# Zero matmuls, a scheduler that follows TensorE's clock, and a new order of the early work in a hybrid encoder block

## The chip, the cores and the metric

The kernel runs on one core of a Trainium2 chip. The metric is the device time of one execution in microseconds (us). Each program is run several times and the median is given. TensorE (PE) does the matrix products, VectorE (DVE), ScalarE (ACT) and GpSimd (POOL) the elementwise work, and SyncE (SP) issues most transfers. The clock of PE that the chip grants has two levels here, 1.2 and 2.4 GHz; the profile gives it as a share, 0.50 or 1.00.

## What is computed

One layer of a streaming encoder on 1024 tokens of width 1024, in float32. The reference, cut to what matters:

```python
def block(x, mem, ...):
    h = rms_norm(x, g_mix)
    cq, ckv, krope, gate, u = split(h @ w_in)          # 256, 128, 32, 512, 512 columns
    q = rms_norm(cq, g_cq) @ w_uq                      # 8 heads, 64 + 32 rotary
    k, v = split(rms_norm(ckv, g_ckv) @ w_ukv)         # 8 heads, 64 each
    a = block_causal_attention(rope(qk_norm(q)), rope(qk_norm(k, krope)), v)
    r = rg_lru(u, conv_w, ...) * gelu(gate)            # conv, gates, linear scan in time
    x = x + concat(rms_norm(a), rms_norm(r)) @ w_out
    x = x + mem_cross_attention(rms_norm(x), rms_norm(mem), ...)
    return x + hier_moe(rms_norm(x), ...)              # 32 experts, 2 of 8 in the best group
```

The recurrent part, which the text comes back to, is `a = exp(-8 r softplus(-lam))`, `b = sqrt(1 - a*a) * (i * xc)` and the scan `h[t] = a[t] h[t-1] + b[t]`, with `r` and `i` sigmoids of two small block-diagonal products of `xc`.

## The kernel before, in words

A float32 product is made of three matmuls on values split into a high and a low part (`mm3`): names that end in `h` and `l` are such parts, and ACT makes the high part while DVE makes the low one (`evac_split`). The tokens are cut in eight tiles `t` of 128; attention takes them in four pairs `pr`. The stages are:

- the in-projection: `zb` gives `z` (the latents q and kv and the rotary key) for every tile, `pr` the eight column blocks of the recurrent part (`rnn_x`, `rnn_u`);
- `prep(t)`: `pcT` transposes a tile of `z`, `pk`, `pq` and `pv` are the up-projections, then the norm of q and k in `qs` and `kn`, the rotation of `qs` by the tables `tab`, and `pqT`, eight transposes each of `kn` and of `qs`, which give `kTh`, `kTl`, `qTh` and `qTl`;
- `step(s)`: one step of attention over a head of a pair. `at_max` forms scores `pS` and their row maxima `nm` on DVE; `at_row` transposes the maxima (`pnm`), which ACT writes to `nT` and a DMA puts into a row of `qT`; `at_exp` forms scores in the transposed form, `pST`, which ACT turns into `PT`; `at_pv` gives `po`, which DVE divides into `oa`; `at_out` norms a finished pair and transposes it (`poT`);
- `rnn_gates_end(c)`: the gate products `pg` of column block `c`, and behind them a chain over ACT and DVE (`ra`, `ri`, `tl`, `sq`), the scan, `gt` and the sum of squares; `rnn_ss` takes the sum of squares over the tokens by matmuls with ones (`pss`);
- the out-projection, cross-attention to the memory, the routing, and the experts, whose weights are loaded, split and multiplied.

The order of all that is not the order of the code. `body` runs the functions above once and records every operation in `Prog.ops`, with its engine, an assumed duration and what it depends on. The sequence of the recording is `PLAN`, a string of short names: `w` is `mla_w` (loads and splits of `w_uq` and `w_ukv`), `x`, `u` and `g` with a number are `rnn_x`, `rnn_u` and the gates of a column block, `z` is `mla_z`, `p` is `prep`, `s` is `step`, `q` is `rnn_ss`, `k` `mem_k`, `r` `rnn_out`, `o` `outproj_w`, `t` the out-projection of a token tile, `T` and `R` are `x1_T` and `x1_r`, the transposes and the row sums of the result, and `v` is `mem_v`. Then `Prog.order` makes a list schedule: it lets a clock run, and whenever an engine is free it takes the recorded operation with the lowest number that is ready and may start (`can`). An operation may not start when the tiles it opens do not fit: there are 49 large slots, 24 small ones, and 8 banks of PSUM (`CAPS`). `LAT` holds the assumed hand-over times between engines. What comes out is the instruction order of each engine, and the hardware then waits for the true dependences. The table `ON` says for which tiles an elementwise operation of `prep` is on DVE; the others are on POOL.

All instructions are issued by one helper (L156 before, L160 after the change), so the rows are told apart by the tiles they write and read.

Of the kernel before, what the change touches and what calls it, by code (L numbers as in the profile page):

```python
# [9 lines left out]
F32 = mybir.dt.float32  # L10
F32R = mybir.dt.float32r
BF = mybir.dt.bfloat16
# [6 lines left out]
P = 128  # L19
# [11 lines left out]
    LAT[_e, "SP"] = LAT["SP", _e] = 0.2  # L31


AHEAD, AHEAD_SPLIT, AHEAD_LOAD, AHEAD_MOE, THR = 30.0, 24.0, 30.0, 4.0, 3.0


# [74 lines left out]


class _Op:
    __slots__ = ("eng", "cost", "emit", "deps", "succ", "tiles", "i", "ahead", "wait", "dma", "keep", "t0", "thr", "port")


class Prog:
    def __init__(self, tc, pools):
        self.tc, self.pools, self.ops, self.direct = tc, pools, [], False
        self.ahead = AHEAD  # L120
        self.n = 0
        self.after = None
        self.hold = None
        self.fast = False

    def tile(self, kind, shape, dt, name):
        t = _Tile(kind, list(shape), dt, name)
# [15 lines left out]
    def op(self, eng, cost, fn, args, kw, outs, ins, dma=0.0):  # L143
        def emit():
            for v in outs + ins:
                if v.t.real is None:
                    self.alloc(v.t)
            a = [x.real() if isinstance(x, _View) else x for x in args]
            k = {}
            for n, x in kw.items():  # L150
                if isinstance(x, _View):
                    x = x.real()
                elif isinstance(x, tuple) and x and x[0] == "ix":
                    x = bass.IndirectOffsetOnAxis(ap=x[1].real(), axis=0)
                k[n] = x
            return fn(*a, **k)  # L156
        if self.direct:
            return emit()
        o = _Op()
        o.eng, o.cost, o.emit, o.dma, o.i = eng, cost, emit, dma, len(self.ops)  # L160
        o.ahead, o.deps, o.succ, o.tiles, o.keep, o.thr = self.ahead, {}, [], [], 0, 1e9


        src = [v for v in ins if v.t.kind not in ("p", "d") and _free(v) > 1]
        o.port = not dma and (eng == "POOL" or eng == "DVE" and (len(src) > 1 or self.fast))
        for w, vs in ((False, ins), (True, outs)):
            for v in vs:
                t = v.t
                if t.kind == "p":
                    box = (0, P, 0, 1 << 30)  # L170
                else:
                    box = (v.p0, v.p1, int(v.idx.min()), int(v.idx.max()) + 1)
                for (j, wj, bx) in t.acc:
                    if (w or wj) and j != o.i and box[0] < bx[1] and bx[0] < box[1] and box[2] < bx[3] and bx[2] < box[3]:
                        o.deps[j] = True
                if w:
# [12 lines left out]
        return o  # L189


    def order(self):
# [63 lines left out]
            return True  # L256

        held = []
        while len(result) < n:
            held.clear()  # L260
            progress = True
            while progress:
# [4 lines left out]
                for e in engs:  # L267
                    if free[e] > now + 1e-9 or not (ready[e] or e == "SP" and loads):
                        continue
                    tried, pick = [], None  # L270
                    while pick is None and ready[e] and len(tried) < 40:
                        i = heapq.heappop(ready[e])
                        if can(ops[i]):
                            pick = i
                            break
                        tried.append(i)
                    for i in tried:
                        heapq.heappush(ready[e], i)
                    if pick is None and e == "SP" and loads and can(ops[loads[0]]):
                        pick = heapq.heappop(loads)  # L280
                    if pick is None:
                        continue
                    o = ops[pick]
                    for t in o.tiles:
                        if t.kind in CAPS and id(t) not in have:
                            have.add(id(t))
                            live[t.kind] += 1
                            N[t.kind][f:t.first] += 1
                    started[pick] = True
                    o.t0 = now  # L290
                    result.append(o)
                    while f < n and started[f]:
                        f += 1
                    end = now + o.cost
                    if o.port:
# [13 lines left out]
            while fin and fin[0][0] <= now + 1e-9:  # L309
# [8 lines left out]
                for s in o.succ:  # L318
# [6 lines left out]
        self.makespan = now  # L325
        return result

    def flush(self):
# [28 lines left out]
class _PE(_Engine):  # L357
    def matmul(self, o, lhsT, rhs, start, stop, **kw):
        n = _free(o)
        dt = rhs.dt  # L360
        c = max(0.109, n / 2246.0 + 0.004) if dt == F32R else (2 * max(0.109, n / 1123.0) if dt == F32 else max(0.027, n / 2246.0))
        return self._do("matmul", (o, lhsT, rhs), dict(start=start, stop=stop, **kw), c)

    def transpose(self, o, i, ident):
        return self._do("transpose", (o, i, ident), {}, 0.109)


# [49 lines left out]
for _name, _w in [("g_mix", 8), ("conv_w", 16), ("conv_b", 4), ("b_rg", 4), ("b_ig", 4), ("lam", 4),  # L417
# [3 lines left out]
    _n += _w  # L421
NPAR = _n

ON = {"qr": 4, "kr": 4, "ke": 0, "tm": 0, "qc": 8}

PLAN = """w x0 x1 x2 u0 g0 u1 g1 u2 z g2 p0 x3 p1 u3 s0 p2 s1 s2 s3 p3 s4 s5 s6 p4 s7 s8 s9 p5 s10 s11 s12 g3 s13 s14 s15
    q s16 s17 s18 s19 s20 s21 p6 p7 s22 s23 s24 s25 s26 s27 s28 s29 s30 s31 s32 k s33 s34 s35 s36 o s37 r t3 t0 t2  # L430
    s38 t7 t1 R0 T0 T1 t5 T2 T3 t4 t6 v R1"""
NROW = 224 * P
FAR = 8192

# [1 line left out]
def body(tc, A, out_ap):  # L436
# [243 lines left out]
    for t in range(NT):  # L680
# [2 lines left out]
        z.append(z_t[:, t % 2, :])  # L683
        SC.activation(z[t], acc[t], AF.Copy, scale=rx[:, t:t + 1])
    row_bcast(Rb, rx)


    ord_ = prog.tile("d", [4 * P, SEQ], F32, "ord")
# [706 lines left out]
    for t in range(NT):  # L1395
# [3 lines left out]
        for k in range(KC):  # L1399
            PE.matmul(pX[k // 4][:, k % 4 * P:k % 4 * P + P], XN[t][:, k * P:(k + 1) * P], sel0[0][:, t, :],  # L1400
                      start=t == 0 and k % 4 == 0, stop=t == NT - 1 and k % 4 == 3, skip_group_check=True)


    idx = Cn([P, 32], I32, name="idx")
    gts = Cn([P, 64], F32, name="gts")
# [240 lines left out]
```

## Time and profile before

| | us |
|---|---|
| median of 3 runs | 1132.08 (1131.44 to 1136.94) |
| the profiled execution | 1131.79 |
| its span | 1129.8 |
| mean granted clock of PE | 0.980 |

The profile comes from one execution, in which the time from the first to the last instruction, the span, is 1129.8 us. A row of a timeline is: start in us from the span's start, duration, engine, line, operation, output and inputs by their names, shapes, and the number of instructions of that kind in a row; in brackets the idle time of the engine just before, and what ended it. Durations of PE's matmuls overlap, since they are pipelined: what a matmul costs is the distance to the next one's start. In the 40 slices of the page each digit is the busy share of 28.2 us in tenths.

### The profile page before, as it was taken

What the parts mean: (1) busy time and instruction counts of PE and PEld (TensorE: products, weight loads), DVE (VectorE), ACT (ScalarE), POOL (GpSimd) and SP (SyncE); (2) the same over time, 40 slices, a digit from 0 to 9 for tenths busy, and PEclk for the clock granted to TensorE, in tenths of its full rate; (3) what the DMA queues carried; (4) which work ended last, traced back from release to release, by engine and by line L of the source; (5) the groups of instructions that cost most, each with busy time, mean ns of one, the idle gap of its engine ahead of it and who ended that gap; (6) DMA issues with size and microseconds to landing.
All of it is one profiled execution on the core that took longest, in us unless ns stands there. A gap on an engine that the chain in (4) does not pass through costs nothing. (4 is left out here: it accounts for less than half of the span.)

```text
span 1129.8 us, 16959 instructions
## 1 busy us (share of the span) xinstructions
PE 1084.4 (96%) x6013; PEld 926.3 (82%) x6014; DVE 787.6 (70%) x1692; ACT 685.3 (61%) x1163; POOL 181.8 (16%) x231
## 2 busy tenths in 40 slices
PE   7999999899999999999999999999999999998993
PEld 7988778899998988898888889889888777775762
DVE  5567899858763713454764356676999999997982
ACT  6837866636554612433492334443888888987982
POOL 1100023203000000000000121024333223233111
PEclk9999999779999999999999998999999999999997
DMA  9401100000443120352235627448899999989991
GB/s 345 186 19 38 57 1 1 19 2 2 169 161 138 34 98 20 128 190 75 75 150 186 211 75 243 149 150 288 296 330 333 332 322 315 320 305 305 327 307 32
DMA packets 61220, 190.18 MB, mean 168 GB/s; under 512 B 11121, under 2 KB 11906, under 8 KB 61131
## 3 DMA queue, kind: packets, MB, share of 16 engines
q1 hardware_dynamic: 52058, 172.48, 42.6%
q0 software_dynamic: 9072, 16.58, 6.0%
q8 instruction: 48, 0.79, 0.3%
q14 instruction: 42, 0.34, 0.1%
HBM read 174.00 MB, written 31.46 MB: 182 GB/s over the span
## 5 line engine op out<-in xcount | busy, mean ns | idle before, releaser
L156 DVE TENSOR_TENSOR wel<-wer,weh 128x1024 fp32r<-128x1024 f32 x192 | 228.0, 1222 | 21.1 <-ACT weh L156 17.7
L156 ACT ACTIVATE weh<-wer 128x1024 fp32r<-128x1024 f32 x192 | 196.1, 1063 | 14.4 <-DMA wer<-in_w_dn 7.9
L156 PE MATMUL pgu<-wel,xgTh 128*128 128x512 f32 x256 | 107.1, 418 | 7.2 <-DVE wel L156 7.1
L156 PE MATMUL pgu<-weh,xgTh 128*128 128x512 f32 x256 | 103.2, 403 | 0.7 <-ACT weh L156 0.6
L156 PE MATMUL pgu<-weh,xgTl 128*128 128x512 f32 x256 | 101.5, 396 | 0.0
L156 POOL DMA_INDIRECT out<-y,idx x32 | 55.0, 1718 | 221.8 <-DMA out<-y,idx 67.4
L156 PE MATMUL py<-weh,heT 128*128 128x512 f32 x256 | 85.7, 395 | 1.3 <-ACT heT L156 1.1
L156 PE MATMUL po<-V,PT 128*128 128x65 f32 x576 | 73.4, 280 | 0.4 <-DVE qTl L156 0.4
L156 PEld LDWEIGHTS po<-V,PT 128*128 128x128 f32 x576 | 70.7, 199 | 0.7 <-DVE qTl L156 0.6
L156 PEld LDWEIGHTS pgu<-wel,xgTh 128*128 128x128 f32 x256 | 48.2, 188 | 25.5 <-DVE wel L156 16.8
L156 ACT ACTIVATE PT<-pST 128x512 f32<-128x512 f32 (+1 forms) x80 | 42.2, 558 | 38.0 <-PE pST L156 37.0
L156 ACT ACTIVATE junk<-x 128x512 f32<-128x512 f32 x32 | 20.2, 632 | 72.7 <-DVE x L156 44.5
L156 ACT ACTIVATE y<-py,gts 128x512 f32<-128x512 f32 x64 | 43.8, 687 | 29.0 <-PE py L156 26.5
L156 PEld LDWEIGHTS py<-weh,heT 128*128 128x128 f32 x256 | 48.0, 188 | 13.0 <-ACT heT L156 1.3
L156 PEld LDWEIGHTS pgu<-weh,xgTh 128*128 128x128 f32 x256 | 48.1, 188 | 11.3 <-ACT weh L156 1.5
L156 PEld LDWEIGHTS pgu<-weh,xgTl 128*128 128x128 f32 x256 | 48.3, 189 | 7.9 <-DVE xgTl L156 0.4
L156 PE MATMUL py<-wel,heT 128*128 128x512 f32 x128 | 50.7, 396 | 1.7 <-DVE wel L156 1.7
L156 DVE TENSOR_REDUCE nm<-pS 128x1 f32<-128x512 f32 (+3 forms) x96 | 50.4, 550 | 1.7 <-PE pS L156 1.7
L156 PE MATMUL px<-VWh,PXh 128*128 128x512 f32 x128 | 51.1, 399 | 0.0
L156 PE MATMUL px<-VWh,PXl 128*128 128x512 f32 x128 | 51.1, 399 | 0.0
L156 PE MATMUL pqx<-x1Tl,wqh 128*128 128x512 f32 x128 | 50.8, 397 | 0.0
L156 PE MATMUL pqx<-x1Th,wqh 128*128 128x512 f32 x128 | 50.7, 396 | 0.0
(369 smaller groups left out, 2972.4 us busy)
## 6 DMA issues: line engine op xcount, KB each, us to landing
wer<-in_w_gu SPq DMA_DIRECT2D x128, 512.0 KB
wer<-in_w_dn SPq DMA_DIRECT2D x64, 512.0 KB
wqr<-in_w_mq SPq DMA_DIRECT2D x16, 512.0 KB
xt<-in_x SPq DMA_DIRECT2D x8, 512.0 KB
wrr<-in_w_rnn SPq DMA_DIRECT2D x8, 512.0 KB
wkr<-in_w_mk SPq DMA_DIRECT2D x8, 512.0 KB
wor<-in_w_out SPq DMA_DIRECT2D x8, 512.0 KB
x<-in_x SPq DMA_DIRECT2D x8, 512.0 KB
```

The lines of the kernel that those rows point to most:

```text
L156: return fn(*a, **k)
```

## The change

Four things change. A tile of zeros (`fil`, 128 x 128 bf16) and a PSUM tile `pfil` are made, and one matmul of them stands behind the z stage, one at the end of the routing; between the two the planner may repeat the first where PE has found nothing that may start. The planner counts the columns that PE works on (`cols`, four times for float32) in stretches of its own clock; it doubles PE's assumed durations in a stretch that follows one with few of them. `ON["kr"]`, the product of `kn` by its norm, goes from 4 to 6, so it is on DVE for tiles 4 and 5 too. And `PLAN` has another order: `x2` ahead of `w`, `z` ahead of `g1`, `t5` ahead of `t2`, `T0` ahead of `R0`. The core of the diff:

```diff
-        while len(result) < n:
+        win, act, half, slow = 0, {}, False, 0
+        recent = []
+        done = 0
+        while done < n:
...
+                    if e == "PE":
+                        while (win + 1) * WINDOW <= now:
+                            half = act.get(win, 0.0) < LOW * WINDOW
+                            win += 1
+                            slow += half
                     if pick is None:
+                        if e == "PE" and self.fill and started[self.fill[0].i] and not started[self.fill[1]]:
...
+                            if sum(x[1] for x in recent) < KEEP * WINDOW:
+                                d = self.fill[0]
+                                result.append(d)
...
                         continue
...
                     end = now + o.cost
+                    if e == "PE":
+                        end += o.cost * half
...
-ON = {"qr": 4, "kr": 4, "ke": 0, "tm": 0, "qc": 8}
-PLAN = """w x0 x1 x2 u0 g0 u1 g1 u2 z g2 p0 x3 p1 u3 s0 p2 s1 s2 s3 p3 s4 s5 s6 p4 s7 s8 s9 p5 s10 s11 s12 g3 s13 s14 s15
+ON = {"qr": 4, "kr": 6, "ke": 0, "tm": 0, "qc": 8}
+PLAN = """x2 w x0 x1 u0 g0 u1 z g1 u2 g2 p0 x3 p1 u3 s0 p2 s1 s2 s3 p3 s4 s5 s6 p4 s7 s8 s9 p5 s10 s11 s12 g3 s13 s14 s15
...
-    s38 t7 t1 R0 T0 T1 t5 T2 T3 t4 t6 v R1"""
+    t2 s38 t7 t1 T0 R0 T1 T2 T3 t4 t6 v R1"""
...
+    fil = Cn([P, P], BF, name="fil")
+    V.memset(fil, 0.0)
+    pfil = prog.tile("p", [P, 512], F32, "pfil")
+    PE.matmul(pfil[:, :P], fil, fil, start=True, stop=True)
+    d = prog.ops[-1]
+    prog.fill = [d, 0]
...
+    prog.fill[1] = len(prog.ops)
+    PE.matmul(pfil[:, :P], fil, fil, start=True, stop=True)
```

What the change makes of the order of the instructions, at the places that the prediction speaks of (an instruction, its output and inputs with the numbers of the buffers, and the size of the output):

On PE, in the early attention, at the transposes of tile 1 (`kn_1216` and `qs_1244` before, `kn_1220` and `qs_1248` now). Before:

```order
L156 MATMUL pqT_1446<-C_69,kn_1216 99x128 x4
L156 MATMUL pqT_1452<-C_69,kn_1216 99x128 x4
L156 MATMUL pq_1410<-wuql_456,cT_1383 128x384
L156 MATMUL pq_1410<-wuqh_444,cT_1383 128x384
L156 MATMUL pq_1420<-wuqh_434,cT_1383 128x384
...
L156 MATMUL pv_1435<-wukvh_460,cT_1383 128x512
L156 MATMUL pk_1475<-wukvh_460,cT_1399 128x512
L156 MATMUL pk_1475<-wukvl_472,cT_1399 128x512
L156 MATMUL pqT_1480<-C_69,qs_1244 99x128 x4
L156 MATMUL pqT_1486<-C_69,qs_1244 99x128 x4
```

With the change, from the second zero matmul on:

```order
L160 LDWEIGHTS fil_80
L160 MATMUL pfil_554<-fil_80 128x128
L160 MATMUL pS_256_1386<-kTh_1341,qTh_1368 128x128
...
L160 MATMUL pqT_1448<-C_69,kn_1220 99x128 x4
L160 MATMUL pqT_1458<-C_69,kn_1220 99x128 x4
L160 MATMUL pq_1415<-wuqh_435,cT_1388 128x384
L160 MATMUL pq_1415<-wuqh_443,cT_1388 128x384
L160 MATMUL pq_1415<-wuql_456,cT_1388 128x384
L160 MATMUL pqT_1472<-C_69,qs_1248 99x128 x4
L160 MATMUL pqT_1479<-C_69,qs_1248 99x128 x4
L160 MATMUL pq_1415<-wuqh_443,cT_1388 128x384
```

Of the up-projections between the two groups of transposes all but three now come behind the second.

On PE behind the gate products of the last column block (`pg`). `kn_1653` and `qs_1878` before are `kn_1788` and `qs_1885` now. Before:

```order
L156 MATMUL pS_433_2078<-kTh_1345,qTh_1724 128x256
L156 MATMUL pS_433_2078<-kTh_1670,qTh_1724 128x256
L156 MATMUL pST_2083<-qTh_1716,kTh_1337 128x256
...
L156 MATMUL pqT_2133<-C_69,kn_1653 99x128 x4
L156 MATMUL pqT_2138<-C_69,kn_1653 99x128 x4
L156 MATMUL pS_446_2144<-kTh_1345,qTh_1724 128x256
...
L156 MATMUL pqT_2206<-C_69,qs_1878 99x128 x4
L156 MATMUL pqT_2212<-C_69,qs_1878 99x128 x4
L156 MATMUL pnm_2218<-C_69,nm_2029 4x128
```

With the change:

```order
L160 MATMUL pS_438_2095<-kTh_1349,qTh_1735 128x256
L160 MATMUL pS_438_2095<-kTh_1687,qTh_1735 128x256
L160 MATMUL pqT_2104<-C_69,kn_1788 99x128 x4
L160 MATMUL pqT_2112<-C_69,kn_1788 99x128 x4
L160 MATMUL pqT_2123<-C_69,qs_1885 99x128 x4
L160 MATMUL pqT_2129<-C_69,qs_1885 99x128 x4
L160 MATMUL pST_2138<-qTh_1721,kTh_1341 128x256
...
L160 MATMUL pST_2173<-qTh_1721,kTl_1698 128x128
L160 MATMUL pnm_2186<-C_69,nm_1863 4x128
L160 MATMUL pST_2189<-qTh_1721,kTh_1341 128x256
```

Both groups of transposes now stand ahead of the 24 `pST`, and the first `pnm` behind them; a second `pnm` (from `nm_2038`) follows nine `pST` later.

On DVE in the same place, with the change (`ri` by `tl` and the operation that writes `sq_2098`, the scan, are the last of the gate chain):

```order
L160 TENSOR_TENSOR qs_1885<-qs_1885 128x8x32
L160 TENSOR_TENSOR kTl_1964<-pqT_2112,kTh_1946 99x4x128
L160 TENSOR_TENSOR ri_2073<-ri_2073,tl_2051 128x1024
...
L160 SCALAR_TENSOR_TENSOR sq_2098<-ra_2025,ri_2073 128x1024
L160 SCALAR_TENSOR_TENSOR qTl_1994<-pqT_2123,colq_76,qTh_1975 99x4x128
...
L160 TENSOR_TENSOR gt_1427<-sq_2098,gt_1427 128x1024
...
L160 TENSOR_REDUCE nm_1863<-pS_437_2091 128x1
L160 TENSOR_TENSOR sq_922<-sq_922,sq_2098 128x1024
...
L160 TENSOR_REDUCE nm_2038<-pS_438_2095 128x1
```

The maxima `nm` from which the two `pnm` are made stand behind the scan, the two `qTl` and `gt`; before, the first of the pair (`nm_2029`) stood ahead of the scan.

## Rows read from the trace of the kernel before

**Rows 1.** The page: PE's total, and busy tenths and granted clock in slices.

```profile
PE 1084.4 (96%) x6013; PEld 926.3 (82%) x6014; DVE 787.6 (70%) x1692; ACT 685.3 (61%) x1163; POOL 181.8 (16%) x231
...
PE   7999999899999999999999999999999999998993
...
PEclk9999999779999999999999998999999999999997
```

**Rows 2.** Stretches: length, busy us (instructions) by engine, PE's granted clock, DMA share, GB/s.

```profile
150.00:180.00 30.00, 26.80 (x175) 23.40 (x174) 29.32 (x77) 24.37 (x42) 7.91 (x23) 1.00 0.00 1
205.80:213.40 7.60, 6.17 (x55) 6.01 (x53) 5.85 (x11) 7.36 (x11) 1.52 (x7) 1.00 0.00 0
213.40:237.40 24.00, 22.79 (x104) 21.99 (x105) 15.02 (x43) 8.11 (x19) 2.04 (x7) 0.50 0.06 23
```

**Rows 3.** Timeline of PE, 212 to 243 us.

```profile
213.46 0.58 PE L156 MATMUL pST<-qTh,kTh 97*128 97x256 f32 x1 [1.49 <-ACT PT L156]
...
215.55 2.03 PE L156 MATMUL pqT<-C,qs 128*99 128x128 f32 x8 [0.44 <-POOL qs L156]
...
224.80 3.41 PE L156 MATMUL pss<-ones,sq 128*128 128x1 f32 x16
...
228.43 0.41 PE L156 MATMUL pST<-qTh,kTh 97*128 97x256 f32 x1
...
230.88 3.19 PE L156 MATMUL po<-V,PT 128*128 128x65 f32 x14
...
236.86 0.41 PE L156 MATMUL pST<-qTh,kTh 97*128 97x256 f32 x1
...
238.44 1.72 PE L156 MATMUL po<-V,PT 128*128 128x65 f32 x14
...
240.76 0.28 PE L156 MATMUL pST<-qTh,kTh 97*128 97x256 f32 x1
...
242.11 0.61 PE L156 MATMUL po<-V,PT 128*128 128x65 f32 x4
```

**Rows 4.** Timeline of PE, 159 to 164 us.

```profile
159.90 0.50 PE L156 MATMUL pk<-wukvh,cT 128*128 128x512 f32 x1 [2.51 <-DVE cT L156]
...
160.58 1.03 PE L156 MATMUL pqT<-C,kn 128*99 128x128 f32 x8
...
163.44 1.04 PE L156 MATMUL pqT<-C,qs 128*99 128x128 f32 x8
```

**Rows 5.** Timeline of POOL, near 163 us.

```profile
162.91 0.21 POOL L156 COPY qs<-mrow 128x24 f32<-128x24 f32 x1 [2.27 <-DVE qs L156]
```

**Rows 6.** Timeline of DVE, one row near 183 us, then 206 to 220 us.

```profile
182.79 0.69 DVE L156 TENSOR_TENSOR kn<-kn,rqk 128x512 f32<-128x512 f32 x1
...
206.64 1.30 DVE L156 SCALAR_TENSOR_TENSOR tl<-sq,tl 128x1024 f32<-128x1024 f32 x1 [1.06 <-ACT sq L156]
...
208.07 0.68 DVE L156 TENSOR_REDUCE nm<-pS 128x1 f32<-128x512 f32 x1
...
209.28 0.42 DVE L156 TENSOR_TENSOR qs<-qs,tab 128x256 f32<-128x256 f32 x1
...
211.53 1.23 DVE L156 TENSOR_TENSOR ri<-ri,tl 128x1024 f32<-128x1024 f32 x1 [0.90 <-ACT tl L156]
...
213.21 2.28 DVE L156 TENSOR_TENSOR_SCAN sq<-ra,ri 128x1024 f32<-128x1024 f32 x1
217.48 1.60 DVE L156 SCALAR_TENSOR_TENSOR qTl<-pqT,colq,qTh 99x512 fp32r<-99x512 f32 x2 [2.00 <-ACT qTh L156]
219.00 1.22 DVE L156 TENSOR_TENSOR gt<-sq,gt 128x1024 f32<-128x1024 f32 x1
```

**Rows 7.** Timeline of ACT, 205 to 210 us.

```profile
205.08 0.59 ACT L156 ACTIVATE PT<-pST 128x512 f32<-128x512 f32 x1
205.56 1.06 ACT L156 ACTIVATE sq<-ra 128x1024 f32<-128x1024 f32 x1
...
209.15 1.28 ACT L156 ACT_TABLE_LOAD   x1
```

More of the change, by code (lines that the diff above doesn't have):

```diff
@@ L31 @@
     LAT[_e, "SP"] = LAT["SP", _e] = 0.2
+WINDOW, LOW, KEEP = 3.413, 0.34, 0.5
 AHEAD, AHEAD_SPLIT, AHEAD_LOAD, AHEAD_MOE, THR = 30.0, 24.0, 30.0, 4.0, 3.0
@@ L113 @@
 class _Op:
-    __slots__ = ("eng", "cost", "emit", "deps", "succ", "tiles", "i", "ahead", "wait", "dma", "keep", "t0", "thr", "port")
+    __slots__ = ("eng", "cost", "emit", "deps", "succ", "tiles", "i", "ahead", "wait", "dma", "keep", "t0", "thr", "port", "cols")
 class Prog:
@@ L124, in __init__ @@
         self.fast = False
+        self.cols = 0
+        self.fill = None
     def tile(self, kind, shape, dt, name):
@@ L161, in op @@
         o.ahead, o.deps, o.succ, o.tiles, o.keep, o.thr = self.ahead, {}, [], [], 0, 1e9
+        o.cols = self.cols if eng == "PE" else 0
         src = [v for v in ins if v.t.kind not in ("p", "d") and _free(v) > 1]
@@ L280, in order @@
                         pick = heapq.heappop(loads)
-                    if pick is None:
+                    if e == "PE":
[3 more added lines that the diff above has]
+                            slow += half
+                    if pick is None:
+                        if e == "PE" and self.fill and started[self.fill[0].i] and not started[self.fill[1]]:
+                            while recent and recent[0][0] < now - WINDOW:
+                                recent.pop(0)
+                            if sum(x[1] for x in recent) < KEEP * WINDOW:
+                                d = self.fill[0]
+                                result.append(d)
+                                c = d.cost * (2 if half else 1)
+                                free[e] = now + c
+                                recent.append((now, d.cols / 2400.0))
+                                act[win] = act.get(win, 0.0) + d.cols / 2400.0
+                                progress = True
                         continue
@@ L291, in order @@
                     result.append(o)
+                    done += 1
                     while f < n and started[f]:
@@ L294, in order @@
                     end = now + o.cost
+                    if e == "PE":
+                        end += o.cost * half
+                        recent.append((now, o.cols / 2400.0))
+                        act[win] = act.get(win, 0.0) + o.cols / 2400.0
                     if o.port:
@@ L324, in order @@
                         heapq.heappush(soon, (rt[s], s))
-        self.makespan = now
+        self.makespan, self.slow = now, slow
         return result
@@ L361, in matmul @@
         c = max(0.109, n / 2246.0 + 0.004) if dt == F32R else (2 * max(0.109, n / 1123.0) if dt == F32 else max(0.027, n / 2246.0))
+        self.prog.cols = n * (4 if dt == F32 else 1)
         return self._do("matmul", (o, lhsT, rhs), dict(start=start, stop=stop, **kw), c)
     def transpose(self, o, i, ident):
+        self.prog.cols = _free(o)
         return self._do("transpose", (o, i, ident), {}, 0.109)
@@ L422 @@
 NPAR = _n
-ON = {"qr": 4, "kr": 4, "ke": 0, "tm": 0, "qc": 8}
-PLAN = """w x0 x1 x2 u0 g0 u1 g1 u2 z g2 p0 x3 p1 u3 s0 p2 s1 s2 s3 p3 s4 s5 s6 p4 s7 s8 s9 p5 s10 s11 s12 g3 s13 s14 s15
-    q s16 s17 s18 s19 s20 s21 p6 p7 s22 s23 s24 s25 s26 s27 s28 s29 s30 s31 s32 k s33 s34 s35 s36 o s37 r t3 t0 t2
-    s38 t7 t1 R0 T0 T1 t5 T2 T3 t4 t6 v R1"""
+ON = {"qr": 4, "kr": 6, "ke": 0, "tm": 0, "qc": 8}
+PLAN = """x2 w x0 x1 u0 g0 u1 z g1 u2 g2 p0 x3 p1 u3 s0 p2 s1 s2 s3 p3 s4 s5 s6 p4 s7 s8 s9 p5 s10 s11 s12 g3 s13 s14 s15
+    q s16 s17 s18 s19 s20 s21 p6 p7 s22 s23 s24 s25 s26 s27 s28 s29 s30 s31 s32 k s33 s34 s35 s36 o s37 r t3 t0 t5
+    t2 s38 t7 t1 T0 R0 T1 T2 T3 t4 t6 v R1"""
 NROW = 224 * P
```

## The prediction

> **What bounds the kernel now.** I read the page's engine list first, then its slices, then the stretches where a slice shows less than a full TensorE, and there the order of waits engine by engine. PE is busy 1084.4 of 1129.8 us, and in its slices almost every digit is a 9 [rows 1]: it is the bound nearly everywhere, so a change can win only where PE idles or where its clock is low. The PEclk digits show one place: the 7s near 212 to 240 us. The table of stretches takes it apart [rows 2]: from 213.4 to 237.4 the granted clock is 0.50 (the lower level, 1.2 GHz) with PE busy 22.79 of 24.00 us. At the upper level (2.4 GHz) the same matmuls would take half, 11.4 us; that is the largest thing an order of the early work could win here, 1.0% of the span. The 7.6 us ahead of the fall had PE busy 6.17 us only, and the last wait before it is 1.49 us for ACT's PT [rows 2, 3]. The clock came back at 237.4, half a microsecond into a pST group, behind po, poT and pS matmuls without a gap [rows 3].
>
> The page's second loss is in 150 to 180 us, where PE is busy 26.80 of 30 and DVE 29.32: DVE is the bound there [rows 2]. All times below are in the clock of the profiled execution of before, which took 1131.79 us, 0.3 us under the median of the runs shown. The point up to which I compare is the pST at 236.86 [rows 3]; the order on PE behind it is the same for a long way. About 0.5%, 5.7 us, is what a measurement of this kernel can tell from no change: "same" is 1126.4 to 1137.7.
>
> **Zero matmuls.** The planner may repeat the first one when PE has work that may not start, but the order of the built program holds only the two written by hand. The first stands at about 46 us, behind the z stage; the one that ends the filling is ready at once and goes out the first time PE has nothing else, at about 154 us. None stands in a later wait. So the change does not do what its words say: it does not fill PE's idle time, and what remains of it is the order. A 128-column bf16 matmul is not in the trace. From above: eight 128-column transposes last 1.03 us together [rows 4], 0.13 each, two make 0.26. From below it is nothing, where PE waits anyway; no gain, since neither stands near the waits ahead of the fall. I take 0.2, the upper end, for these two places have PE busy. The one PSUM bank of eight that the two hold between them costs nothing I can place: PE is at 9 in every slice from the second to the seventh [rows 1].
>
> **Start and later moves.** One load of the recurrent weights goes one place ahead on SP's queue, and their splits on ACT go ahead of two evacuations of z. The in-projection matmuls fill slices two to five completely [rows 1], so this costs nothing; without that cover it would show as idle time in those slices. The out-projection of token tile 5 and the transposes of x1 behind it move as a block in a stretch where PE is full and at full clock [rows 1]: nothing.
>
> **Stage 155 to 199 us.** The kn products of tiles 4 and 5 move from POOL to DVE, 0.69 us each [rows 6], so DVE, full here, has 1.4 us more to do. And PE reaches the transposes of qs of tile 1 earlier. In before it does the eight of kn at 160.58, then some ten up-projection matmuls, and the eight of qs at 163.44 [rows 4], just when POOL's copy into qs has ended (162.91 + 0.21) [rows 5]. In the new order only three pq matmuls stand between the two. They take some 0.6 us, so PE arrives at 162.0 and waits to 163.4: +1.4. The matmuls that covered this come later, where they cover nothing that was not covered. From below it is nothing, if a later DVE wait was longer by as much and shrinks; from above 3, that wait and DVE's two products one behind the other (1.4 + 1.4 = 2.8). I take +1.4.
>
> **Stage of the gates, 199 to 237 us.** Here the order moves most. In before 24 pST stand ahead of the transposes of the next tile's kn, and 12 more and two po groups ahead of those of qs, which run at 215.55 after 0.44 us of wait [rows 3]. In the new order the transposes of kn and qs stand directly behind the gate matmuls and three pS groups, with the 24 pST behind them. PE gets through kn at about 205.6. But qs is not ready: its chain goes over ACT and DVE. ACT's sq ends at 206.6 in before; one PT of about 0.5 us ahead of it goes [rows 7], so 206.1. Then DVE, word for word in the new order: tl to 207.3, nm to 207.9, qs by tab to 208.3, one kTl (like the kn product, about 0.6) to 208.9, the add on qs to 209.3 [rows 6]; POOL's copy 0.2 [rows 5] and hand-overs: 209.6. **PE idles 4.0 us there**, more than twice the 1.49 us behind which the clock fell in before. So I expect it to fall earlier.
>
> From 209.6 the eight transposes (2.03 at the low clock) and the 24 pST in front of pnm (12 took 228.43 to 230.88, 2.45) are done by 216.5 [rows 3]. That costs nothing by itself, since DVE's chain to pnm is longer: kTl to 210.0, ri by tl 1.2 (its tl comes from ACT behind a table load of 1.28, in time [rows 7]), nm 0.6, the scan 2.2 to 214.2, qTl twice 1.6, gt 1.2 to 217.0, and two nm with small ones 1.5: 218.5 [rows 6]. The first pnm waits for it; the second stands behind one more 1.2 us sum and an nm, and comes at **220.6** (in before the pair of pnm was spread over 217 to 223).
>
> What PE still has from there to the common point, priced at the low clock: three pST 0.6, seven po 3.0 (the row of 14 halves, 230.88), then everything that before does from 224.80 to 236.86 (pss, twelve pST, seven po, poT, pS: 12.06 us), and on top twelve pST 2.45, seven po 3.0 and eleven pS of 0.26: 8.3 [rows 3]. 220.6 + 0.6 + 3.0 + 12.06 + 8.3 = 244.6. But the clock comes back, in before in the pST group right behind poT and pS. The same group stands in the same place here, and behind it are two groups of seven po, two of six pS and one of twelve pST. At the full clock po and pS take 2.32 (238.44 to 240.76) and pST 1.35 (to 242.11) [rows 3], so 2 x 2.32 + 1.35 = 6.0 instead of 11.7. That makes 238.9, **+2.0** against 236.86. The bounds: -4.3, if all from 220.6 is at full clock (24.0 / 2 = 12.0, 232.6), and +7.7, if none is. The middle is nearest to the row of before, in which the clock returned at that group.
>
> **Sum:** 1131.8 + 0.2 + 1.4 + 2.0 = 1135.4 us, behind which nothing changes: PE is the bound to the end, and what it is late it stays late.
>
> On the clock the trace shows a fall behind a row of waits and a return behind dense work, with 24 us between them [rows 2, 3]. The Trainium skill, "TensorE: Matmul & The Clock Gate", section "What's actually happening", says that the watch over the engine's activity runs freely and does not start with the kernel, and that one should not fit to a particular count of cold matmuls, the loss being under 1% of a typical span. By it this change moves the time by 11.3 us at most (1% of 1129.8, an estimate from that page), to 1120.5 or 1143.1, and a planner that counts from its own first instant need not meet the chip's: it speaks for B below, and against A. The trace agrees on the size; on the phase no run here shows anything.
>
> **The rivals.**
> A, faster: the clock does not fall in this stage, or PE waits no longer than before did. Then the 22.79 us become 11.4 and only the first wait and the zeros remain: 1131.8 - 11.4 + 1.6 = 1122.0. It decides if qs is ready within some 1.5 us of kn and the second pnm before about 214. For it: the new order puts work in front of what it waits for, and every wait before the fall was short. Against: the sum of DVE's rows, which says 209.6 and 220.6.
> B, slower: the clock falls and does not return before the common point, +7.7: 1131.8 + 1.6 + 7.7 = 1141.1. The place is the pss and poT matmuls behind 224; it decides if the twelve pST behind them are too few to bring it back, as twelve pST and seven po at 228.43 to 233.9 were too few in before [rows 3]. If the clock falls also at the new wait at 162, close behind the wait of 2.51 us at 157.4 [rows 4], each 2 us at the low clock cost one more; 8 us of it give 1145.
> C, nothing: the clock returns in the 24 pST and stays, the bound from below: 1131.8 + 1.6 - 4.3 = 1129.1.
>
> **How the numbers follow.** The forecast, 1135.4 with a range of its own of 1131 to 1140 (DVE's chain 2 us either way, the first wait 0 to 3), has a chance of 0.42, 0.29 of it under 1137.7. C has 0.15, of which 0.02 falls under 1126.4. A has 0.20 and B 0.23. Faster: 0.20 + 0.02 = 0.22; same: 0.29 + 0.13 = 0.42; slower: 0.13 + 0.23 = 0.36. The range takes in A's 1122 and B's upper end with 1 us at the lower side for the unknown: 1121 to 1145.
>
> **What would show it.** Right: a wait of 1 to 2 us ahead of pqT from qs near 162, one of 3 to 5 us near 206, the granted clock at 0.50 from about 208, pnm released by DVE near 219 and 221, and the full clock back near 234 with some 2 us lost in the stage. Wrong: PE full through 205 to 222 with the clock at 1.00 (A), or 0.50 beyond 240 (B); a zero matmul inside a wait; a difference that arises behind 245 us, above all in the stage of the experts.

## The result and the profile after

The change takes 1140.17 us in the median of 19 runs (1132.11 to 1157.86), before 1133.05 (19 runs of the same sessions, 1128.31 to 1136.94). The ratio is 1.0052, with a 95% interval of 1.0034 to 1.0071. That ratio, like those of the table below, leaves out runs more than 1.5% above the fastest of their kernel; here these runs are the kernel's own doing, as will be seen, so the medians and ranges are of all runs.

The runs fall into two groups: ten from 1132.1 to 1140.2 and nine from 1148.5 to 1157.9, with nothing between. Each run also comes with its span and the mean granted clock of TensorE, and 2 x (1 - clock) x span is the time that it spent at the low clock: 43 to 57 us in the lower group, 78 to 102 in the upper. Some 12 to 16 us of that lie behind PE's last matmul in every run that was profiled, and cost nothing. A straight line through the 19 runs is 1114.1 us + 0.437 us for each us at the low clock, with a correlation of 0.99. So nearly all of the spread goes with the clock. That it costs somewhat less than half its time is probably since waits for other engines don't grow with it; no run tests that.

The profiled execution is one of the upper group: 1155.48 us, span 1153.6, clock 0.958. The engine totals and slices of the page, after the change (to be read against [rows 1]):

```profile
PE 1106.2 (96%) x6015; PEld 946.5 (82%) x6016; DVE 790.5 (69%) x1695; ACT 683.6 (59%) x1163; POOL 183.0 (16%) x229
...
PE   7999989899999999999999999999999999998992
...
PEclk9999989656999999999999999999999999999997
```

PE is as full as before, and the granted clock has a deep place where before had 77, and a first one ahead of it. The table of stretches, after the change (length, busy us by engine, granted clock; against [rows 2]):

```profile
163.00:170.00 7.00, 6.40 (x26) 5.92 (x27) 5.54 (x15) 3.92 (x7) 0.21 (x1) 0.62 0.01 4
...
208.00:220.00 12.00, 8.00 (x32) 6.47 (x33) 10.50 (x15) 7.49 (x11) 2.00 (x3) 0.55 0.00 0
220.00:270.00 50.00, 50.00 (x238) 49.93 (x238) 22.19 (x71) 12.16 (x28) 1.86 (x16) 0.50 0.03 12
...
275.00:285.00 10.00, 10.00 (x54) 9.48 (x54) 6.64 (x20) 7.06 (x13) 0.00 (x0) 0.87 0.00 1
```

From 220 to 270 PE is busy 50.00 of 50 us and stays at 1.2 GHz all the time. Before, the clock was back at 237.4. The timeline of PE, after the change, at the two groups of waits (start, duration, what ended the wait; against [rows 3, 4]):

```profile
160.20 0.50 PE L160 MATMUL pk<-wukvh,cT 128*128 128x512 f32 x1 [2.51 <-DVE cT L160]
160.60 1.20 PE L160 MATMUL pqT<-C,kn 128*99 128x128 f32 x8
...
163.48 2.03 PE L160 MATMUL pqT<-C,qs 128*99 128x128 f32 x8 [0.71 <-POOL qs L160]
...
208.39 0.68 PE L160 MATMUL pqT<-C,kn 128*99 128x128 f32 x4 [1.25 <-POOL kn L160]
210.15 1.17 PE L160 MATMUL pqT<-C,kn 128*99 128x128 f32 x4 [1.08 <-DVE nm L160]
211.76 1.17 PE L160 MATMUL pqT<-C,qs 128*99 128x128 f32 x4 [0.44 <-POOL qs L160]
213.34 1.17 PE L160 MATMUL pqT<-C,qs 128*99 128x128 f32 x4 [0.41 <-DVE kTl L160]
215.00 0.58 PE L160 MATMUL pST<-qTh,kTh 97*128 97x256 f32 x1 [0.49 <-DVE nm L160]
...
217.84 0.58 PE L160 MATMUL pST<-qTh,kTh 97*128 97x256 f32 x1 [1.19 <-DVE qTl L160]
...
221.75 0.41 PE L160 MATMUL pnm<-C,nm 128*4 128x128 f32 x1
```

The eight transposes of kn, 1.03 us at the full clock, are one group of four at 0.68 and from 210 on groups of four at 1.17: the clock falls between 208.4 and 210.2. Further on, the loop that attention runs through (twelve pST, seven po, six pS), after the change:

```profile
236.49 3.19 PE L160 MATMUL po<-V,PT 128*128 128x65 f32 x14
239.44 1.63 PE L160 MATMUL pS<-kTh,qTh 96*128 96x256 f32 x6
240.86 0.41 PE L160 MATMUL pST<-qTh,kTh 97*128 97x256 f32 x1
...
247.69 0.41 PE L160 MATMUL pST<-qTh,kTh 97*128 97x256 f32 x1
...
275.10 1.48 PE L160 MATMUL pcT<-C,z 128*128 128x128 f32 x6
276.24 1.41 PE L160 MATMUL pS<-kTh,qTh 96*128 96x256 f32 x5
277.45 0.46 PE L160 MATMUL pk<-wukvh,cT 128*128 128x512 f32 x1
277.75 0.39 PE L160 MATMUL pk<-wukvl,cT 128*128 128x512 f32 x1
```

One turn of the loop takes 6.83 us (240.86 to 247.69) instead of 3.67 at the full clock [rows 3], five turns long, and the clock comes back only where the next tile's pcT, pS and pk stand. The point of comparison, 236.86 before [rows 3], is the pST at 247.69: +10.8. The low clock behind it costs as much again, and more: the out-projection, by tile name (durations, first and last start), stands like this before

```profile
L156 PE MATMUL pout<-woh,oTh x64: 387/394/479, 382.0 to 475.7; 128*128 128x512 f32 x64
```

and after the change

```profile
L160 PE MATMUL pout<-woh,oTh x64: 387/393/475, 406.7 to 500.3; 128*128 128x512 f32 x64
```

so it is 24.7 us later from its first matmul to its last, and the span is 23.8 longer. Nothing more is lost behind 407 us.

### The profile page after: what moved, and what is told of

The parts are those of the page before. It is cut to its first block, busy times and chain, and to the rows that moved or that the text cites. A ratio compares the mean times of both kernels' runs of the same rounds, so it can differ in the third digit from the quotient of the medians.

```text
span 1153.6 us, 16953 instructions
## 1 busy us (share of the span) xinstructions
PE 1106.2 (96%) x6015; PEld 946.5 (82%) x6016; DVE 790.5 (69%) x1695; ACT 683.6 (59%) x1163; POOL 183.0 (16%) x229
## 5 line engine op out<-in xcount | busy, mean ns | idle before, releaser
L160 POOL DMA_INDIRECT out<-y,idx x32 | 60.6, 1895 | 218.4 <-DMA out<-y,idx 55.7
L160 PE MATMUL po<-V,PT 128*128 128x65 f32 x576 | 80.5, 298 | 0.0
L160 PEld LDWEIGHTS po<-V,PT 128*128 128x128 f32 x576 | 78.1, 216 | 0.1
L160 PEld LDWEIGHTS pgu<-wel,xgTh 128*128 128x128 f32 x256 | 48.4, 189 | 24.6 <-DVE wel L160 16.0
L160 PE MATMUL pST<-qTh,kTh 97*128 97x256 f32 (+1 forms) x160 | 49.4, 309 | 1.7 <-DVE qTl L160 1.2
```

## The experiments

There were two theories. **Theory 1**: the time goes with how long PE is at its low clock, and what the change does is to the clock. **Theory 2**: parts of the change cost by themselves (early loads and splits, the products on DVE, zeros and the bank), and the spread comes from outside the order. The table has all runs; S is the planner's clock with the two zeros, K the kn products on DVE, P the new PLAN. A zero in the rows from 4 on is a matmul of zeros put in by hand; run 3 has the two zeros of S without the clock. The last column counts the runs with more than 58 us at the low clock.

| kernel | median us | lowest to highest | ratio to before (95%) | us at the low clock | over 58 |
|---|---|---|---|---|---|
| the change (S, K, P) | 1140.17 | 1132.11 to 1157.86 | 1.0052 (1.0034 to 1.0071) | 43 to 102 | 9 of 19 |
| 1: S and K | 1136.60 | 1131.51 to 1154.35 | 1.0026 (1.0007 to 1.0046) | 41 to 92 | 3 of 12 |
| 2: S and P | 1141.07 | 1132.12 to 1151.96 | 1.0068 (1.0030 to 1.0106) | 32 to 78 | 6 of 12 |
| 3: K, P and the two zeros | 1131.81 | 1130.70 to 1149.00 | 0.9992 (0.9980 to 1.0004) | 34 to 73 | 1 of 12 |
| 7: S alone | 1147.55 | 1132.21 to 1149.29 | 1.0115 (1.0072 to 1.0159) | 43 to 71 | 4 of 6 |
| 4: before, 25 zeros | 1125.84 | 1124.44 to 1130.14 | 0.9932 (0.9915 to 0.9949) | 23 to 34 | 0 of 6 |
| 5: the change, dense piece | 1138.54 | 1136.64 to 1140.97 | 1.0053 (1.0035 to 1.0072) | 48 to 55 | 0 of 7 |
| 6: the change, true filling | 1129.73 | 1125.35 to 1150.42 | 0.9963 (0.9945 to 0.9981) | 16 to 74 | 4 of 12 |
| 8: before, 40 zeros | 1123.40 | 1121.31 to 1130.10 | 0.9936 (0.9914 to 0.9958) | 13 to 29 | 0 of 9 |
| 9: before, 45 zeros | 1122.94 | 1121.38 to 1124.44 | 0.9916 (0.9903 to 0.9929) | 16 to 20 | 0 of 5 |
| 10: before, 7 zeros | 1130.65 | 1127.55 to 1143.89 | 1.0014 (0.9985 to 1.0042) | 34 to 71 | 2 of 12 |
| 11: before, thin piece | 1139.53 | 1129.10 to 1142.97 | 1.0050 (1.0023 to 1.0077) | 43 to 66 | 8 of 12 |
| 12: before, 25 zeros elsewhere | 1137.46 | 1134.64 to 1139.40 | 1.0047 (1.0034 to 1.0061) | 43 to 52 | 0 of 6 |

Before, run beside the first four of these, had 38 to 57 us at the low clock in 29 runs; beside the others it had 36 to 57 in 44 more.

### Which part of the change it is (1, 2, 3, 7)

Run 1 takes the PLAN of before:

```diff
-PLAN = """x2 w x0 x1 u0 g0 u1 z g1 u2 g2 p0 x3 p1 ...
+PLAN = """w x0 x1 x2 u0 g0 u1 g1 u2 z g2 p0 x3 p1 ...
```

> The change with the PLAN of before; the planner's clock, the zeros and the kn products stay as changed. Its order behind the gates is that of the change: the transposes of kn and qs directly behind each other, ahead of 24 pST. Theory 1 (the time goes with how long PE stays at its low clock, and this order makes it fall early, behind waits near 208 us, and keeps it low for an uncertain time): as the change, 1132 to 1158, median near 1140, granted clock 0.956 to 0.981, waits in front of pqT between 206 and 215. Theory 2 (the order of the early loads and splits costs time by itself): back near before, 1131 to 1135.

Run 2 puts the products back on POOL:

```diff
-ON = {"qr": 4, "kr": 6, "ke": 0, "tm": 0, "qc": 8}
+ON = {"qr": 4, "kr": 4, "ke": 0, "tm": 0, "qc": 8}
```

> The change with the kn products of tiles 4 and 5 back on POOL. The planner then puts the transposes of qs behind 24 and 12 more pST, as before. Theory 1: the long low stretch is gone, 1128 to 1137, median within 3 of before, all runs within 0.7%, granted clock 0.978 to 0.985. Theory 2 (the new PLAN costs): still 3 to 8 above before. A third, that the two products on DVE cost by themselves, gives only 1.4 less than the change.

Run 3 takes the doubling out:

```diff
-                            half = act.get(win, 0.0) < LOW * WINDOW
+                            half = False
```

> The change with the planner's doubling of PE's durations taken out; PLAN, zeros and the kn products on DVE stay. The transposes of qs go back behind the pST. Theory 1: near before, 1128 to 1138, no run above 1142, though DVE has its 1.4 us more (so that costs 0 to 1.4). Theory 2: as the change, some runs above 1145.

Run 7 has the doubling and the two zeros alone, with PLAN and `ON` of before:

> The kernel before with only the planner's clock (and the two zero matmuls) added; PLAN and the kn products as before. With the earlier runs all three other pairs of parts are known. Theory 1: the doubled durations alone make the orders in which the return is missed, so some runs above 1145, as with the change less its kn products. If it takes the clock and another part together: all runs 1129 to 1138.

Run 1 has long runs as the change has, so the early loads and splits are not what makes them. Run 2 was the surprise: with the transposes of qs back behind the pST, 6 of 12 runs were long all the same. So theory 1 in its first form, that the two groups of transposes side by side make the long runs, fell; and so did the products on DVE as the cause. The median of run 2, 8.0 us above before, is what theory 2 had for the new PLAN; run 7, which is long without that PLAN, takes this reading away. Run 3 is back at before, but one run of 12 took 1149.00, where theory 1 had none above 1142. Run 7 settles the part: the planner's clock, with the two zeros that run 3 has too, makes 4 of 6 runs long. With it, 22 of 49 runs were long (the change, 1, 2 and 7); without it 1 of 12 (run 3), and none of before.

In the profiles of these orders the clock falls between 206 and 218 us in every case (before: at 213.4), and all four of them are of short runs, in which it is at the low level for 17 to 27 us and then back. Run 1 tells most, for behind the gates its order on PE is that of the change. The timeline of PE and the stretches of its profiled run (1132.59 us), to be held against the rows of the change above:

```profile
232.92 0.41 PE L160 MATMUL pST<-qTh,kTh 97*128 97x256 f32 x1
...
234.11 0.28 PE L160 MATMUL pST<-qTh,kTh 97*128 97x256 f32 x1
...
240.74 0.28 PE L160 MATMUL pST<-qTh,kTh 97*128 97x256 f32 x1
```

```profile
206.00:234.00 28.00, 23.62 (x104) 21.89 (x105) 18.70 (x42) 13.93 (x25) 3.11 (x9) 0.51 0.05 20
234.00:260.00 26.00, 26.00 (x219) 25.77 (x219) 17.48 (x56) 10.59 (x21) 1.82 (x15) 1.00 0.00 1
```

The clock comes back at 234.0, in the pST group right behind poT. In the profiled run of the change the same group, 234.03 to 236.49, runs at the low clock to its end. So one order gives both: the order alone does not settle the return. The table of stretches of run 3 (1130.70):

```profile
216.00:238.00 22.00, 20.63 (x100) 20.36 (x100) 12.04 (x39) 6.82 (x16) 1.41 (x7) 0.53 0.06 25
```

and of run 7 (1132.21), which has, like the change, a first fall near 160 us:

```profile
163.00:170.00 7.00, 6.83 (x33) 6.19 (x32) 4.98 (x12) 5.18 (x9) 0.00 (x0) 0.73 0.01 4
214.00:232.00 18.00, 16.31 (x74) 15.08 (x75) 13.29 (x35) 7.12 (x17) 1.81 (x5) 0.53 0.08 30
```

So it is not the fall that makes a run long. The new form of theory 1 was that the long runs miss the return. Two experiments put that to the test from both sides.

### The return (5, 11)

A helper inserts zero matmuls ahead of the first real matmul into a bank (`t.real`; `z` is a tile of zeros). The real one overwrites them, so neither the order nor a bank changes:

```diff
+                        if k:
+                            self.alloc(t)
+                            z = self.zero.t.real
+                            for _ in range(k):
+                                self.tc.nc.tensor.matmul(t.real[:, :512], z[:, :P], z[:, 0:1].to_broadcast([P, 512]), start=True, stop=True)
                 o.emit()
```

Run 5 is the change with 16 of them ahead of the pST behind poT:

> The change with 16 matmuls of zeros (512 columns each) in one piece ahead of the first group of twelve pST behind poT, near 232 us, in the bank that these pST overwrite. Nothing else moves. Theory 1 in its new form (the clock falls near 210 in every order; what makes the long runs is that it misses its return there and then stays low through the loop of twelve pST, seven po, six pS, which is without gaps but does not bring it back): a dense piece brings it back every time. The piece costs 3.4 at the full clock to 6.8 at the low one; all runs 1133 to 1143, none above 1145. Theory 2 (something outside the order keeps the clock low in some runs): the spread stays and every run is 3 to 7 later, up to 1162.

All seven runs lie from 1136.64 to 1140.97, with 48 to 55 us at the low clock; the upper group is gone. The timeline of PE in run 5 has the piece, and its table of stretches the clock:

```profile
233.59 4.35 PE L375 MATMUL pST<-fil 128*128 128x512 bf16 x16
```

```profile
208.00:236.00 28.00, 24.40 (x105) 21.18 (x105) 19.20 (x44) 13.32 (x24) 1.87 (x8) 0.52 0.05 20
236.00:246.00 10.00, 10.00 (x81) 9.09 (x80) 4.19 (x15) 2.15 (x4) 0.47 (x4) 1.00 0.00 0
```

By the price of the expectation sixteen at the low clock would be 6.8 us; they take 4.35, and the clock is back at 236, so it comes back inside them.

Run 11 does the opposite to the kernel before: 16 zeros of one column (`t.real[:, :1]`) behind the first two poT, ahead of a pS, near 234 us.

> The counterpart of the dense piece: the kernel before with 16 zero matmuls of one column each between the transposes poT and the pS behind them, near 234 us, just ahead of where the clock came back. They keep PE busy 3.4 us at the low clock and do next to nothing, as the pss do in the change's order, directly ahead of poT. Theory 1 (what is missed is the return): the time splits as with the change: some runs at 1134 to 1140, some above 1145, with 70 us or more at the low clock. If the return does not depend on what runs there: all runs 3 later than before, 1132 to 1140.

Its price was mis-sized: the 16 take 0.61 us, not 3.4. The time splits all the same, but by less than theory 1 had it, with no run above 1145. Four runs are at 1129 to 1134, as before, and eight at 1139 to 1143, with 59 to 66 us at the low clock. The timeline of PE and the stretches of the profiled run 11 (1141.79 us):

```profile
234.75 0.61 PE L353 MATMUL pS<-fil 128*128 128x1 bf16 x16
...
261.82 0.29 PE L159 MATMUL pST<-qTh,kTh 97*128 97x128 f32 x1
```

```profile
214.00:235.00 21.00, 19.67 (x97) 18.81 (x98) 13.06 (x38) 6.38 (x14) 2.04 (x7) 0.50 0.07 26
235.00:262.00 27.00, 27.00 (x141) 27.00 (x138) 11.29 (x35) 6.54 (x14) 0.70 (x6) 0.50 0.01 1
262.00:272.00 10.00, 10.00 (x66) 9.47 (x65) 6.16 (x17) 7.07 (x14) 0.63 (x5) 1.00 0.01 3
```

Before came back at 237.4 in its profile; with 0.6 us of thin work just ahead of that point this run stays low to about 262, with PE busy 27.00 of 27. So the order before is safe by little, and it takes no new order to make it miss. Theory 2 has no place for either result. Whether it is the thinness of the 16 or only that everything behind them comes 0.6 us later was not separated: no run put a plain delay of that length there. And the clock comes back, at the row of 261.82, in two groups of twelve pST side by side, which the profiled run of the change went through from 268.38 to 272.11 without a return. So the loop can bring the clock back; it does so in one run and not in another.

### The fall (4, 8, 9, 10, 12)

Run 4 puts 25 zeros into PE's waits behind the gates, in the kernel before:

> The kernel before with 25 matmuls of zeros (512 columns, 0.21 us each at the full clock, 5.3 in all) where PE waits or would wait: 7 ahead of the pS at 211.4, 5 ahead of the transposes of qs at 215.5, 6, 4 and 3 ahead of the pS at 218.5, 223.6 and 224.2. They go into banks that the next real matmul overwrites, so no order and no bank changes. Theory 1: the clock does not fall at 213.4, the 24 us at 0.50 become some 14 to 15, and the time is 1121 to 1125. If activity does not hold the clock, the zeros are paid, partly at the low clock: 1133 to 1140.

The time is 1125.84, just above the 1121 to 1125 of theory 1, and the stage is at full clock, but in the profiled run (1130.14, the longest of the six) the clock fell elsewhere. Its stretches:

```profile
185.00:195.00 10.00, 8.89 (x41) 8.39 (x42) 7.90 (x23) 5.30 (x9) 4.43 (x10) 0.66 0.01 2
210.00:240.00 30.00, 29.03 (x233) 25.75 (x231) 25.06 (x66) 16.96 (x34) 3.41 (x17) 1.00 0.05 18
```

Run 12 has as many zeros where PE does not wait:

> The kernel before with 25 zeros of 512 columns ahead of two tiles of the out-projection, where PE is full and at full clock. This is their price where they hide behind no wait and hold no clock: 25 times 0.21 is 5.3, so 1137 to 1138 in the median, with as much time at the low clock as before. If zeros help by themselves, in any place: 1126 to 1132.

There they cost 6.0 us against the before of that session (1137.46 to 1131.44), 43 to 52 us at the low clock as ever. So the gain of run 4 is not from zeros as such. Run 10 has only the first seven:

> The kernel before with the first 7 of the 25 zeros only (1.5 us, ahead of the pS at 211.4, where PE waits 1.49 us behind it). Theory 1: if the one wait at 212 brings the clock down, 1123 to 1127 as with 25. If the later short waits (0.44, 0.71 and those that appear when PE is fast) bring it down as well, it falls some us later and the time is 1128 to 1133.

This is the second case. The timeline of PE and the stretches of run 10:

```profile
211.06 1.69 PE L353 MATMUL pS<-fil 128*128 128x512 bf16 x7
215.15 1.12 PE L159 MATMUL pqT<-C,qs 128*99 128x128 f32 x8 [1.11 <-POOL qs L159]
217.32 0.62 PE L159 MATMUL pS<-kTh,qTh 96*128 96x256 f32 x3 [0.95 <-ACT nT L159]
```

```profile
210.00:219.00 9.00, 6.77 (x45) 5.02 (x44) 6.60 (x8) 5.37 (x10) 1.58 (x3) 1.00 0.00 0
219.00:234.00 15.00, 14.62 (x70) 14.62 (x71) 8.80 (x36) 4.01 (x9) 0.46 (x4) 0.52 0.09 36
```

The wait of 1.49 us is gone, the next ones are longer (1.11 and 0.95, where before had 0.44 and 0.71), and the clock falls behind those, at about 219. Two of the 12 runs have 66 and 71 us at the low clock, as runs that miss the return have; neither was profiled. Run 8 adds 15 zeros to the 25; eleven go into an open sum of pk with `start=False`, which adds zero to it:

> The kernel before with the 25 zeros from before and 15 more: 11 added to an open sum of pk where PE waits 2.5 us at 157.4, 3 and 1 ahead of the transposes of kn and qs at 184.4 and 186.7 (waits of 0.85 and 0.37), where the clock fell in the profile of the run with 25. Theory 1: that fall goes too; 1122 to 1126, granted clock about 0.990, every run under 1128. If the fall near 187 is not from these waits: as with 25, 1124 to 1130, or 1 later for the zeros.

The profile of run 8 has the full clock through the whole early attention:

```profile
150.00:240.00 90.00, 86.33 (x629) 76.09 (x627) 80.34 (x222) 59.99 (x108) 22.60 (x65) 1.00 0.02 7
```

The median, 1123.40, is as expected, but not every run is under 1128: two of nine, 1128.24 and 1130.10, have 25 and 29 us at the low clock, so a fall is left somewhere in some runs. Run 9 adds five at pk near 138 us:

> The kernel before with the 40 zeros and 5 more, added to the open sum of pk near 138 us, where PE still waits 1.12 us. Theory 1: little low clock is left to win there (the best profile so far has 0.50 only at its idle end, and 2 us near 695), so 1121 to 1126 as with 40, median 1123 and perhaps fewer runs above 1126. If the earlier wait is what started the falls in the slower of those runs, every run is under 1125.

All five runs lie within 1121.38 to 1124.44. Its stretches leave low clock to some 3 us near 693 us and to the idle end:

```profile
690.00:697.00 7.00, 7.00 (x50) 7.00 (x50) 5.85 (x26) 5.10 (x11) 1.27 (x1) 0.76 0.71 269
0.00:1100.00 1100.00, 1077.42 (x6046) 915.61 (x6047) 785.99 (x1692) 680.57 (x1161) 181.93 (x229) 1.00 0.49 173
1100.00:1121.00 21.00, 3.07 (x12) 2.18 (x12) 1.02 (x2) 1.66 (x4) 3.10 (x2) 0.65 0.14 20
```

This version is the fastest of all: 0.9916 of before (0.9903 to 0.9929), 8.5 us. Whether the five are what holds the last two runs of 8 is open, with five runs to nine.

### The change as its words say (6)

Run 6 lets the planner fill where PE's list is empty, and ties the last zero to the last matmul ahead of it:

```diff
-                    if free[e] > now + 1e-9 or not (ready[e] or e == "SP" and loads):
+                    if free[e] > now + 1e-9 or not (ready[e] or e == "SP" and loads
+                                                    or e == "PE" and self.fill and started[self.fill[0].i]
+                                                    and not started[self.fill[1]]):
...
     PE.matmul(pfil[:, :P], fil, fil, start=True, stop=True)
+    prog.ops[-1].deps[max(o.i for o in prog.ops[:-1] if o.eng == "PE")] = True
```

> The change made to do what its words say: the planner may repeat the zero matmul also when PE's list of ready work is empty, and the last zero matmul waits for the end of the routing. The order now holds 85 zero matmuls of 128 columns, 24 of them near 155 to 160 us and 40 near 210 to 225, and one PSUM bank less for the rest up to 700 us. Theory 1: the clock holds through more of the waits than in the change, median 1125 to 1135; the spread shrinks if the return near 235 is not missed. Theory 2 (the zeros and the bank cost more than they hold): 1136 to 1145.

With 85 zeros in the order eight runs are at 1125 to 1131, with 16 to 36 us at the low clock, and four at 1145 to 1150, with 66 to 74. The profiled run (1127.25) has the fall between 215 and 225 still:

```profile
215.00:225.00 10.00, 8.26 (x74) 7.47 (x73) 9.57 (x22) 6.59 (x13) 0.47 (x4) 0.83 0.13 53
```

So the filling, made to work, is worth some 9 us against the change, each median taken from the before of its sessions. A fall that it lets through can still miss its return (the four long runs were not profiled, and are told by their time at the low clock), and the order by the planner's clock is still one that does.

## Why the prediction was right, and where it was not

The time lies in the range given, near the value of rival B (1141.1), and 4.8 us above the forecast of 1135.4. There is luck in that. The median of 19 is the slowest of the ten runs of the lower group, and the next run up, 1148.47, is outside the range; had one of the ten been long, that would have been the median. The prediction had one time with rivals beside it, where the kernel has two groups of runs. The ten of the lower group, 1132 to 1140 with a median of 1136.4, fit the forecast and its own range of 1131 to 1140; the nine of the upper group are rival B, which was priced too low. None of the ten was profiled. What stands for them is run 1's profile: fall at 206.7, return at 234.0, and the pST of the common point at 240.74, 3.9 later than before where the forecast's terms give 3.6. That closeness is in part chance: the first pg is 0.4 late there, where 1.6 was forecast, and the rest, 3.5, arises in the stage, where 2.0 was.

- **Zeros, 0.2.** Right. Two stand in the trace, at 46.21 and 154.76, and neither in a wait. The pk behind the 2.51 us wait starts at 160.20 instead of 159.90 [rows 4]; the zeros and the start together are at most that 0.3.
- **Start and later moves, nothing.** Right as far as the runs show: run 1 undoes them and keeps the long runs, and from the first out-projection matmul on the offset stays as it is (24.7 us at the first and 24.6 at the last).
- **Stage 155 to 199, +1.4.** The wait ahead of the transposes of qs is there, but 0.71 long and not 1.4. A fall here, which the forecast had put under rival B, is there in the profiled run: the clock is 0.62 in 163 to 170. It begins at 161.5, ahead of the new wait, so it is not that wait that brings it down. The first pg starts at 201.13 instead of 199.12; that is +2.0, low clock included, where 1.6 was forecast with the zeros.
- **Gates: qs ready at 209.6, PE idle 4.0 us.** Right in size, wrong in form. PE waits 4.9 us in six pieces between 207 and 218 (1.25, 1.08, 0.44, 0.41, 0.49 and 1.19). The first stands ahead of kn already: the DVE product that K moved there took 1.42 us beside a POOL product, twice the 0.69 of [rows 6], and POOL's kn by rk behind it 1.59, to 208.3. What lengthened it is not shown: the other product that moved, at 193.35, took 0.68 with POOL at work beside it too. The timelines of DVE and of POOL, after the change:

```profile
205.07 1.42 DVE L160 TENSOR_TENSOR kn<-kn,rqk 128x512 f32<-128x512 f32 x1
```

```profile
204.47 1.47 POOL L160 TENSOR_TENSOR qs<-qs,rqk 128x768 f32<-128x768 f32 x1 [3.00 <-issue]
...
206.75 1.59 POOL L160 TENSOR_TENSOR kn<-rk,rqk 128x256 f32<-128x256 f32 x1
```

- **The first pnm at 218.5.** With the offset of 1.6 that is 220.1; it stands at 221.75, and the second at 223.88 (220.6 and 1.6 give 222.2). The releaser was wrong: DVE's `nm` for the first is done at 220.9, and PE comes to the pnm out of the pST in front without a wait. DVE acts ahead of that, in the waits for `nm` and `qTl` at 215.00 and 217.84, which the forecast let the pST run through. The timeline of DVE, after the change:

```profile
220.37 0.54 DVE L160 TENSOR_REDUCE nm<-pS 128x1 f32<-128x384 f32 x1
```

- **The clock comes back in the pST group behind poT, +2.0.** This is the step that failed, in nine runs of 19. It was read from one return in one profile of before, as though the same groups in the same place would always bring it back. Run 1's profile has the return in that group; in the profiled run of the change the group is there, at 234.03, and the clock stays low. At the common point the loss is 10.8, near rival B's 1.6 + 7.7 = 9.3.
- **"The PEclk digits show one place."** The 8 in the 25th slice of [rows 1] was passed over: before's granted clock is 0.83 in 680 to 690 and in 700 to 710 us. Run 1's profile has 1.00 there, and that is most of why its span is only 0.6 us longer than before's in spite of the 3.9.
- **"Behind which nothing changes."** Wrong in the upper group, and this is what B's price lacked. The low clock does not end with the stage: the loop behind it runs 27.4 us more at half speed (247.69 to 275.1), which is 13.7.

The rule that was weighed is from the Trainium skill, "TensorE: Matmul & The Clock Gate", section "What's actually happening": the watch over the engine's activity runs freely and does not start with the kernel. The runs fit it, since one program has 43 us at the low clock in one run and 102 in another, and a planner's own count does not tell what a run will do; that the phase is the cause no run shows. The under 1% of a typical span in that section of the Trainium skill is its figure for the ramp, the cold matmuls at a kernel's start. The prediction took it as a bound for a fall in mid-kernel too, and as that it fails: by the line through the runs, 102 us at the low clock cost 25 us more than 45, 2.2% of the span.

What stays open is why the return comes in one run and not in another of the same order, and which feature of the planner's orders makes it uncertain. They have the thin pss and the poT close together, or po between poT and the next pST, and run 11 shows that 0.6 us are enough; but no run moved poT alone.

## What to carry to other kernels

A clock that falls can cost twice: in the stretch that it falls in, and in all that runs behind it until it comes back, and the same work may bring it back in one run and not in another. So look for where it returns, not only for where it falls, and see how near to a miss that return is, over many runs and not in one profile: the mean granted clock of each run gives the time spent at the low level. Work of no use cost 6.0 us where PE was full, and paid for itself in waits that were there anyway; written into the bank that the next matmul overwrites, or added as zero to an open sum, it needs neither a bank nor a new order; here 45 such matmuls gave back 8.5 us, while the scheduler that follows the clock by its own count made orders with more long runs.

## What the runs showed that was not expected

- PE can be busy without a gap, 50.00 of 50 us, and stay at 1.2 GHz throughout; busy share alone does not tell the clock.
- The runs of one program on one core split into groups with nothing between them (1132 to 1140 and 1148 to 1158), and the profile that was taken shows one of them.
- 0.61 us of one-column matmuls turned the kernel before, 1131.44 in that session, into one of 1139.53 in the median.
- One loop, without a gap in either, brought the clock back in run 11 and not in the profiled run of the change.
- Filling one wait of 1.49 us with seven zeros moved the fall by some 6 us and hardly the time: the engine then waits longer at the next two places.
